# A first load of b as two loads of one slice each, and a first cast shared by two engines, in a matmul-GELU-matmul kernel on Trainium2

## The chip, the cores and the metric

The kernel runs on one core of one Trainium2 chip. That core has a matrix engine (PE, with its weight loads shown apart as PEld), a vector engine (DVE, VectorE), a scalar engine (ACT, ScalarE), GpSimd (POOL) and a sync engine (SP), each with an instruction queue of its own, and DMA engines that move data between the chip's memory (HBM) and the core's memory. Instructions of different queues are ordered by semaphores only. The metric is the device time of one execution in microseconds (us). The kernel before the change takes 117.73 us, the median of three runs that lie between 117.45 and 117.9 us.

## What is computed

```python
def reference(a, b, c):                     # a 1024x1024, b 1024x2048, c 2048x1024, float32
    h = np.matmul(a, b)
    h = 0.5 * h * (1 + np.tanh(np.sqrt(2 / np.pi) * (h + 0.044715 * h ** 3)))
    return np.matmul(h, c).astype(np.float32)
```

## The kernel before

The kernel keeps h transposed, as two halves `hT[0]` and `hT[1]` of 512 rows of a each. For that it needs a transposed (`aT`, bf16, by half h and by contraction slice k of 128; there are eight slices) and b in bf16 (`b1` for its first 1024 columns, `b2` for the rest). A matmul takes a slice of b, 128x128, as its weights and a slice of `aT`, 128x512, as the moving operand, and adds up the eight slices in one bank of PSUM.

The work has three parts. The first (lines 229 to 287) makes the first four column tiles of h for both halves with plain matmuls. The other columns of h and the whole second product go through `seven`, a Strassen-like scheme with seven block products in place of eight, whose sums VectorE and ScalarE work out. The last part writes the output, in tiles of 128 rows by 512 columns, through `store` (line 428).

The change touches the start. There, five loads are issued on SP's queue (lines 75 to 79), in this order: a's first quarter of columns for half 0 (`sta[:, 0, 0]`, 512 KB), b's contraction slices 0 and 1 (`stb[:, 0:2]`, 512 KB in one load), a's first quarter for half 1 (`sta[:, 1, 0]`, 512 KB), a's second quarter for half 0 (`sta[:, 0, 1]`, 512 KB), and b's slice 2 (`stb[:, 2]`, 256 KB). They arrive as float32. All further loads go through GpSimd's queue (lines 85 to 104), which casts to bf16 on the way; GpSimd issues none of them before it has copied one element of the first load of a (`gate`, line 81). While nothing has arrived, the matrix engine multiplies zeros (`stir`, line 122).

The order on each engine is the order of the program, written out by hand. Around the change it is this:

- `cast_a(0, 0, nc.vector)` (line 230) casts a's first load into a bf16 tile `ab`, in one VectorE instruction for all 256 columns (line 110).
- `turn(0, 0, 4, ab)` (lines 138 to 147) makes two steps, one for each contraction slice n: four 128x128 transposes on the matrix engine (line 145), then one VectorE copy of the result into `aT` (line 146). The generator is advanced with `next(tn)`, so that other work can be put between its steps.
- `cast_b(0, nc.vector, nc.vector, nc.scalar)` (line 233) casts b's slice 0 in three pieces of columns, of 128, 128 and 256; `cast_b(1, nc.scalar)` (line 236) casts slice 1 in one ScalarE instruction (line 108).
- `cast_a(1, 0, nc.vector, nc.scalar)` (line 237) casts a's load for half 1 in two pieces of 128 columns, VectorE's for the first slice and ScalarE's for the second.
- `block(0, range(4), (0,))` and `block(0, range(2), (1,))` (lines 238 and 239) are six matmuls (line 114). Then come the eight transposes for half 1 (line 240), and so on slice by slice, alternating with loads that GpSimd has brought.

The change also touches the end of the program text: `done2` (line 431) stores an output tile in one transfer of 256 KB or in two of 128 KB. Before, the tiles j = 1 and j = 2 of the first group, (i, l) = (0, 0), go in two. With five loads and 19 stores, SP issues 24 transfers. Tiles named `ot` that wait to be stored share four buffers (line 302).

Of the kernel before, what the change touches and what calls it, by code (L numbers as in the profile page):

```python
# [19 lines left out]
def kernel(ctx, tc, a, b, c, out):  # L20
    nc = tc.nc
# [3 lines left out]
    H = 512  # L25
# [4 lines left out]
    bv = b.rearrange("(kt p) n -> p kt n", p=128)  # L30
# [9 lines left out]
    def slot(tag, shape, dt, name):  # L40
        return big.tile(shape, dt, name=name, tag=tag)

    def bank(i, shape=(128, H), dt=F32, name="ps"):
        return pp.tile(list(shape), dt, name=name, tag=f"bank{i}", padded_shape=None)

    def pieces(tag, bufs, shape, dt, name):
        return small.tile(shape, dt, name=name, tag=tag, bufs=bufs)
# [17 lines left out]
    stb = slot("x0", [128, KT, H], F32, "stb")  # L65
# [3 lines left out]
    def a_part(h, q):  # L69
        return av[:, 4 * h:4 * h + 4, ds(q * 256, 256)]  # L70

    def b_part(q):
        return bv[:, 2 * q:2 * q + 2, 0:H]

    nc.sync.dma_start(out=sta[:, 0, 0], in_=a_part(0, 0))  # L75
    nc.sync.dma_start(out=stb[:, 0:2], in_=b_part(0))  # L76
    nc.sync.dma_start(out=sta[:, 1, 0], in_=a_part(1, 0))
    nc.sync.dma_start(out=sta[:, 0, 1], in_=a_part(0, 1))
    nc.sync.dma_start(out=stb[:, 2], in_=bv[:, 2, 0:H])
# [19 lines left out]
    for n in range(2):  # L99
        for k in range(0, KT, 4):  # L100
            nc.gpsimd.dma_start(out=b2[:, k:k + 4, ts(n, H)],
                                in_=bv[:, k:k + 4, ds(1024 + n * H, H)])
# [3 lines left out]
    def copy(eng, dst, src):  # L106
        if eng is nc.scalar:
            nc.scalar.activation(dst, src, AF.Copy)
        else:
            nc.vector.tensor_copy(dst, src)  # L110
# [11 lines left out]
    def stir(*widths):  # L122

        for w in widths:
            nc.tensor.matmul(ps[0, 3][:, 0:w], warm[:, 0:128], warm[:, 0:w],
                             start=True, stop=True, skip_group_check=True)

    def cast_a(h, q, *engs):

        ab = pieces("ab", 2, [128, 4, 256], BF16, "ab")  # L130
        for i, eng in enumerate(engs):
            w = 256 // len(engs)
            for j, e in enumerate(eng if isinstance(eng, tuple) else (eng,)):
                m = slice(2 * j, 2 * j + 2) if isinstance(eng, tuple) else slice(0, 4)
                copy(e, ab[:, m, ts(i, w)], sta[:, h, q][:, m, ts(i, w)])
        return ab

    def turn(h, q, i, ab):

        banks = i if isinstance(i, tuple) else (i,)  # L140
        pts = [bank(x, (128, 2, H), BF16, "pt") for x in banks]
        for n in range(2):
            pt = pts[n % len(pts)]
            for m in range(4):
                nc.tensor.transpose(pt[:, n, ts(m, 128)], ab[:, m, ts(n, 128)], ident)  # L145
            nc.vector.tensor_copy(aT[:, h, 2 * q + n], pt[:, n])  # L146
            yield
# [79 lines left out]
    one = Seven(4, quarters(b2, 0, H), BB, [None] * 4, zero.t)  # L227

    stir(256, 256, 256, 256, 256)
    tn = turn(0, 0, 4, cast_a(0, 0, nc.vector))  # L230
    next(tn)
    stir(128)
    cast_b(0, nc.vector, nc.vector, nc.scalar)
# [15 lines left out]
    tn = turn(0, 1, 7, ab)  # L249
# [4 lines left out]
    for q in range(1, 3):  # L254
        k = 2 * q
        block(0, range(4), (k,))
        tn = turn(1, q, 7, abq[:, q, 1])
# [5 lines left out]
        tn = turn(0, q + 1, 7, abq[:, q + 1, 0])  # L263
# [10 lines left out]
    tn = turn(1, 3, 0, abq[:, 3, 1])  # L274
# [153 lines left out]
    def store(mt, q0, w, ot, eng=None):  # L428
        (eng or nc.sync).dma_start(out=out[ts(mt, 128), ds(q0, w)], in_=ot)

    def done2(i, l, j, p):
        if (i, l) == (1, 0):
            ot = pieces("o", 4, [128, H], F32, "ot")
            nc.vector.tensor_copy(ot, p)
            p = ot
        n = 2 if (i, l) == (0, 0) and j else 1
        for q in range(n):
            r = ds(q * (H // n), H // n)
            store(4 * i + j, l * H + q * (H // n), H // n, p[:, r])

    def between2(n):
# [12 lines left out]
        elif n == "P73":  # L454
            two.t4(two.t[1], 4)

    seven(two, done2, between2)


# [28 lines left out]
```

## Time and profile before

| what | value |
|---|---|
| time, median of three runs (lowest, highest) | 117.73 us (117.45, 117.9) |
| span of the profiled execution, first to last instruction | 115.7 us |
| median time less that span | 2.0 us |
| matrix engine busy | 111.1 us, 96% of the span |
| VectorE, ScalarE, GpSimd busy | 90.0, 51.4, 17.2 us |
| granted clock of the matrix engine | 1.000 |
| first instruction that uses a's first load | 4.40 us |
| first product matmul | 6.83 us |

The profile is of one execution. Its page gives the span of that execution, 115.7 us, but no time of its own for what lies around the span; the table therefore sets the span beside the median of the runs. Times inside a profile count from the start of the span. A line of the timeline gives start, duration, engine, source line, operation, the tile written and the tile read, and in brackets how long the engine had been idle and what ended that. The chain of waits follows the work that ended last back to the start. Rows by window give, after the length, the busy time and the number of instructions of PE, PEld, DVE, ACT and POOL in that stretch, then the granted clock, the mean share of the DMA engines in use, and the GB/s moved.

### The profile page before, as it was taken

What the parts mean: (1) busy time and instruction counts of PE and PEld (TensorE: products, weight loads), DVE (VectorE), ACT (ScalarE), POOL (GpSimd) and SP (SyncE); (2) the same over time, 40 slices, a digit from 0 to 9 for tenths busy, and PEclk for the clock granted to TensorE, in tenths of its full rate; (3) what the DMA queues carried; (4) which work ended last, traced back from release to release, by engine and by line L of the source; (5) the groups of instructions that cost most, each with busy time, mean ns of one, the idle gap of its engine ahead of it and who ended that gap; (6) DMA issues with size and microseconds to landing.
All of it is one profiled execution on the core that took longest, in us unless ns stands there. A gap on an engine that the chain in (4) does not pass through costs nothing.

```text
span 115.7 us, 1461 instructions
## 1 busy us (share of the span) xinstructions
PE 111.1 (96%) x542; PEld 77.1 (67%) x542; DVE 90.0 (78%) x107; ACT 51.4 (44%) x86; POOL 17.2 (15%) x29
## 2 busy tenths in 40 slices
PE   7989999999999999999999999999999999999980
PEld 6645555546776447888885444688888888888860
DVE  0347748789999998935699999999999986954770
ACT  5053000999259997166698429500124982000000
POOL 2497755223322000000000000000000000000000
PEclk9999999999999999999999999999999999999999
DMA  2999999999999999998000000060000002014993
GB/s 69 295 381 229 200 199 205 204 208 205 206 211 209 212 213 209 212 210 168 8 0 0 6 0 0 38 235 0 0 0 0 0 4 91 1 73 176 370 363 106
DMA packets 13414, 15.94 MB, mean 138 GB/s; under 512 B 736, under 2 KB 9312, under 8 KB 13408
## 3 DMA queue, kind: packets, MB, share of 16 engines
q0 software_dynamic: 8672, 9.31, 47.6%
q1 hardware_dynamic: 4736, 6.56, 15.8%
q8 instruction: 4, 0.07, 0.3%
q14 instruction: 2, 0.02, 0.0%
HBM read 20.97 MB, written 4.19 MB: 218 GB/s over the span
## 4 chain that ended last, share of the span: by engine, by line
PE 90%; DMA 5%; SPq 1%; DVE 1%; issue 0%
PE ps L212 76%; PE ps L114 11%; DMA sta<-in_a_dram 5%; PE pt L145 3%; SPq L76 0%; DVE ab L110 0%; SPq L75 0%; DVE ot L375 0%
## 5 line engine op out<-in xcount | busy, mean ns | idle before, releaser
L212 PE MATMUL ps<-x,s 128*128 128x512 f32 x128 | 29.6, 391 | 0.0
L212 PEld LDWEIGHTS ps<-x,s 128*128 128x128 f32 x128 | 24.0, 188 | 5.1
L212 PE MATMUL ps<-x,x 128*128 128x512 f32 x96 | 22.9, 394 | 0.0
L212 PEld LDWEIGHTS ps<-x,x 128*128 128x128 f32 x96 | 18.0, 188 | 3.9
L114 PE MATMUL ps<-aT,b 128*128 128x512 bf16 x64 | 16.1, 379 | 0.2 <-DVE b L110 0.2
L298 ACT ACTIVATE v<-ps 128x512 f32<-128x512 f32 x10 | 6.0, 599 | 19.1 <-PE ps L212 19.1
L212 PE MATMUL ps<-c_sb,hT 128*128 128x512 bf16 (+1 forms) x72 | 14.2, 356 | 0.0
L212 PE MATMUL ps<-x 128*128 128x512 f32 x56 | 13.2, 392 | 0.0
L212 PEld LDWEIGHTS ps<-x 128*128 128x128 f32 x56 | 10.2, 188 | 2.6 <-ACT u L298 0.4
L118 ACT ACTIVATE hT<-ps 128x512 bf16<-128x512 f32 x14 | 7.3, 595 | 9.7 <-PE ps L114 9.7
L212 PEld LDWEIGHTS <-hT 128*128 128x128 bf16 x72 | 6.9, 98 | 7.0 <-issue 0.5
L118 ACT ACTIVATE hT<-ot 128x512 bf16<-128x512 f32 x18 | 10.4, 624 | 2.0 <-DVE ot L303 2.0
L212 PE MATMUL ps<-aT,b 128*128 128x512 bf16 x48 | 10.7, 379 | 0.0
L146 DVE COPY aT<-pt 128x512 bf16<-128x512 bf16 x16 | 6.7, 423 | 5.1 <-PE pt L145 5.1
L303 DVE TENSOR_TENSOR ot<-ps,u 128x512 f32<-128x512 f32 x10 | 6.7, 690 | 5.1 <-ACT u L298 5.1
L303 DVE TENSOR_TENSOR ot<-ps,v 128x512 f32<-128x512 f32 x10 | 6.7, 688 | 4.8 <-DMA out_dram<-ot 3.8
L170 DVE TENSOR_TENSOR x<-c_sb 128x1024 fp32r<-128x1024 bf16 x8 | 9.3, 1226 | 0.0
L114 PEld LDWEIGHTS <-b 128*128 128x128 bf16 x64 | 5.7, 98 | 4.5 <-DVE b L110 0.3
L212 PEld LDWEIGHTS <-b 128*128 128x128 bf16 x48 | 4.6, 98 | 5.7 <-issue 0.3
L104 POOL DMA_DIRECT2D c_sb<-in_c_dram x8 | 5.6, 702 | 13.1 <-DMA b<-in_b_dram 12.4
L170 DVE TENSOR_TENSOR x<-b 128x1024 fp32r<-128x1024 bf16 (+1 forms) x4 | 7.0, 1752 | 0.6 <-issue 0.6
L298 ACT ACTIVATE u<-ps 128x512 f32<-128x512 f32 x10 | 5.9, 598 | 3.4 <-PE ps L212 3.2
(44 smaller groups left out, 111.3 us busy)
## 6 DMA issues: line engine op xcount, KB each, us to landing
c_sb<-in_c_dram POOLq DMA_DIRECT2D x8, 512.0 KB, 20.0
out_dram<-ot SPq DMA_DIRECT2D x13, 256.0 KB, 2.1
b<-in_b_dram POOLq DMA_DIRECT2D x6, 512.0 KB, 15.3
sta<-in_a_dram SPq DMA_DIRECT2D x3, 512.0 KB, 6.1
abq<-in_a_dram POOLq DMA_DIRECT2D x5, 256.0 KB, 7.9
out_dram<-ot SPq DMA_DIRECT2D x6, 128.0 KB, 2.0
stb<-in_b_dram SPq DMA_DIRECT2D x1, 512.0 KB, 5.3
b<-in_b_dram POOLq DMA_DIRECT2D x2, 256.0 KB, 8.2
```

The lines of the kernel that those rows point to most:

```text
L104: nc.gpsimd.dma_start(out=c_sb[:, t:t + 2], in_=cv[:, t:t + 2])
L114: nc.tensor.matmul(p, b1[:, k, ts(t, 128)], aT[:, h, k], start=(k == 0), stop=(k == KT - 1))
L118: nc.scalar.activation(hT[h][:, t], p, AF.Gelu_apprx_tanh)
L145: nc.tensor.transpose(pt[:, n, ts(m, 128)], ab[:, m, ts(n, 128)], ident)
L146: nc.vector.tensor_copy(aT[:, h, 2 * q + n], pt[:, n])
L170: nc.vector.tensor_tensor(out=dst[:, r], in0=x[:, r], in1=y[:, r], op=op)
L212: nc.tensor.matmul(p[:, ds(c0, w)], l[:, k, ts(j, 128)], r[:, k, ds(c0, w)], start=(start and k == 0), stop=(k == self.kt - 1), skip_group ...
L298: nc.scalar.activation(st, p, AF.Copy)
L303: nc.vector.tensor_tensor(out=ot, in0=p, in1=st, op=ADD)
```

## The change

```diff
     nc.sync.dma_start(out=sta[:, 0, 0], in_=a_part(0, 0))
-    nc.sync.dma_start(out=stb[:, 0:2], in_=b_part(0))
+    for k in range(2):
+        nc.sync.dma_start(out=stb[:, k], in_=bv[:, k, 0:H])
     nc.sync.dma_start(out=sta[:, 1, 0], in_=a_part(1, 0))
...
-    tn = turn(0, 0, 4, cast_a(0, 0, nc.vector))
+    tn = turn(0, 0, 4, cast_a(0, 0, nc.vector, nc.scalar))
...
-        n = 2 if (i, l) == (0, 0) and j else 1
+        n = 2 if (i, l, j) == (0, 0, 1) else 1
```

b's slices 0 and 1 come in two loads of 256 KB, one behind the other, in the place of the one of 512 KB; each has its own semaphore, so that slice 0 can be used before slice 1 is there. a's first load is cast in two pieces of 128 columns, the first by VectorE and the second by ScalarE, where it was one VectorE instruction of 256 columns. The output tile j = 2 of the first group is stored in one transfer in the place of two, so SP still issues 24 transfers: six loads and 18 stores.

## The prediction

> **What bounds the kernel now.** I read the chain of waits first, because the change sits in the first 8 us of a span of 115.7 us, and only a chain tells whether those count. Its pieces in order of time:
>
> ```profile
> 1.24 0.50 SPq L76
> 1.73 0.05 issue
> 1.78 6.10 DMA sta<-in_a_dram
> 7.88 0.02 issue
> 7.90 0.44 DVE ab L110
> 8.34 0.05 issue
> 8.38 0.62 PE pt L145 x8
> ...
> 24.46 87.96 PE ps L212 x400
> ```
>
> From 8.38 us on there is nothing but the matrix engine up to 112.42. So a change at the start moves the time only by moving 8.38. What ends last before it is not b's load, which the change splits, but a's load for half 1 (line 77): in use at 7.90, cast in 0.44, transposed at 8.38.
>
> The timeline from 4 to 8.5 us says the same from the side of the matmuls:
>
> ```profile
> 4.40 0.69 DVE L110 CAST ab<-sta 128x1024 bf16<-128x1024 f32 x1 [4.40 <-DMA sta<-in_a_dram]
> ...
> 6.54 0.36 DVE L110 CAST b<-stb 128x128 bf16<-128x128 f32 x2 [0.53 <-DMA stb<-in_b_dram]
> 6.83 1.47 PE L114 MATMUL ps<-aT,b 128*128 128x512 bf16 x6 [0.15 <-DVE b L110]
> 7.90 0.43 DVE L110 CAST ab<-sta 128x512 bf16<-128x512 f32 x1 [0.67 <-DMA sta<-in_a_dram]
> ...
> 8.38 0.62 PE L145 MATMUL pt<-ident,ab 128*128 128x128 bf16 x8
> ```
>
> The six matmuls that wait for b end at 6.83 + 1.47 = 8.30, and the transposes behind them on the same queue start at 8.38. They just fit in.
>
> Next question: what sets the arrival at 7.90? Rows by window, the last two numbers the DMA engines' share and the GB/s:
>
> ```profile
> 3.25:3.75 0.50, 0.50 (x3) 0.41 (x2) 0.00 (x0) 0.00 (x0) 0.00 (x0) 1.00 1.12 377
> 3.75:4.25 0.50, 0.50 (x2) 0.40 (x2) 0.00 (x0) 0.00 (x0) 0.00 (x0) 1.00 0.73 236
> 4.25:5.75 1.50, 1.43 (x9) 0.84 (x8) 0.86 (x2) 0.00 (x0) 1.32 (x2) 1.00 0.97 272
> 5.75:7.25 1.50, 1.11 (x9) 0.76 (x8) 0.95 (x4) 0.71 (x2) 1.50 (x4) 1.00 1.06 368
> 7.25:8.75 1.50, 1.41 (x12) 0.66 (x11) 0.43 (x1) 0.85 (x2) 1.50 (x3) 1.00 1.11 396
> ```
>
> The DMA engines are full from 4.25 on. SP issues the five loads within 0.74 to 3.38 us; they are in use at 4.40, 6.54, 7.90, 9.42 and 9.98, about 1.4 us per 512 KB later on. The loads stand in line; it is bytes that a's second load waits for, not its issue. One thing stands out: b's own stretch, 3.75 to 5.75, runs at some 263 GB/s, where the stretches behind it run at 368 and 396.
>
> GpSimd's loads come behind these: in the DMA view from 5.2 to 9 us all packets are on the sync queue, though GpSimd issued its first load at 5.08. And the matrix engine has little to spare there. Its own timeline, and below it that of its weight loads:
>
> ```profile
> 15.07 1.03 PE L114 MATMUL ps<-aT,b 128*128 128x512 bf16 x4
> 15.93 0.39 PE L145 MATMUL pt<-ident,abq 128*128 128x128 bf16 x4
> ```
>
> ```profile
> 15.88 0.26 PEld L145 LDWEIGHTS <-abq 128*128 128x128 bf16 x4 [0.28 <-DMA abq<-in_a_dram]
> ```
>
> The weight load of those transposes waits 0.28 us for a GpSimd load and starts at 15.88; the matrix engine is free at 15.93. So only 0.05 us could be gained at 8.38 without the whole line of loads moving too.
>
> **The change, part by part.**
>
> *Cast of a's first load in two pieces.* Out goes one VectorE cast of 0.69 us; in come a VectorE cast of 128x512 (the row at 7.90: 0.43) and a ScalarE cast of the same size (0.63 in the row of that engine at 7.90), side by side. They end at 4.83 and 5.03 instead of 5.09. The stirs hold the matrix engine to 0.78 + 4.30 = 5.08 (first group of the timeline), so the first transposes move from 5.15 to about 5.10. ScalarE is idle then (4.30 us before 6.54), so its piece costs nothing. GpSimd's one-element copy lasted 0.70 us, from 4.43 to 5.13, as long as the VectorE cast beside it; if it follows the shorter cast, GpSimd issues 0.26 us earlier, into the same line behind the sync queue: 0.
>
> *Slice 0 of b on its own.* b's bytes move from about 3.75 to 5.75 and are in use 0.79 us after that. Half the bytes are there at 4.75, so slice 0 is in use near 5.55. VectorE is then copying the first transposes (5.5 to 5.95, 0.42 each), and casts slice 0's two pieces in 0.36 behind it. The first matmul starts near 6.15, 0.7 us earlier than 6.83. Slice 1 is in use at 6.54 as before, ScalarE's cast of it takes 0.61, and the two matmuls on it follow near 7.2 and are done at about 7.8 (0.59 for two, as in the row at 8.84 of the matrix engine). Then the matrix engine waits for a's second load until 8.38. The wait of 0.08 us (8.30 to 8.38) becomes one of some 0.6, and the time gained for b is given back there: 0. VectorE's queue holds the copy of the second transposes behind the casts, done near 6.75, well ahead of 7.90. The cover that hides it all is a's second load; were that load 0.6 us earlier, the gain would be real.
>
> *One more issue on SP.* The new issue costs what line 79's load of one slice does, 0.55 us, plus 0.05 between issues: 0.60 for the three loads behind it. a's second load is issued at 2.38 instead of 1.78. The first load was issued at 0.74 and bytes flowed at 1.75 to 2.00 (41 GB/s), about 1.1 us later. So a's second load is ready near 3.5, and its turn in line comes at 5.75: margin 2.2 us, cost 0. The ends: 0, and 0.60 were it the issue that counts.
>
> *The line itself.* The trace holds no two loads of b one behind the other there. Lower end: a load of a single slice does run at full rate (line 79's lies in the stretch of 396 GB/s). Were b's slow stretch due to its two-slice form, 0.524 MB would take 1.42 us at 368 GB/s instead of 1.99 at 263, and everything behind would come 0.57 earlier. Upper end: one more turn from load to load. The turn from a's first load to b's cost (377 - 236)/377 x 0.5 us = 0.19; the turns later on show no dip. I take 0: the nearest row in place and data is b's own stretch, and GpSimd's two-slice loads of b show no sign that two slices are slow. The range keeps -0.57 and +0.19.
>
> *The store.* One issue of 256 KB replaces two of 128 KB near 76 us. The `ot` buffer it frees is not written again before 93.83, and landing takes 2.1 us for the one size and 2.0 for the other: 0. The last stores and the count of 24 are unchanged.
>
> The sum against the profiled execution: 115.7 + 0 - 0 = 115.7 us of span, with 2.0 us around it (117.73 - 115.7; the profile gives no time of its own for that execution): 117.7.
>
> *Rules of the Trainium skill.* The trace shows loads that overlap: line 79's 256 KB land 7.1 us after their issue but are in use only 0.56 us after the load ahead of them (9.98 against 9.42). The page "DMA: Bandwidth & Descriptors", section "Anatomy of one DMA — SWDGE (gpsimd) path", puts a fixed cost of about 2.0 us on each DMA, and its section on measured bandwidth says to batch to at least 1 MiB; paid in line, that rule would make this change 2.0 us slower, 119.7. The measured 0.56 decides against it. The same page, section "Queues, rings and completion order", says that a DMA engine takes turns between queues packet by packet; the view from 5.2 to 9 us shows packets of the sync queue alone. By that rule an earlier GpSimd issue would cost the sync loads bandwidth.
>
> **The rivals.**
>
> 1. *b's load gets faster in two pieces* (117.16). For it: the slow 263 GB/s, and one-slice loads that do not show it. Against it: the stretch may be slow because of when it runs. If it holds, a's second load is in use at 7.33 and the transposes start at 7.81, just behind the matmuls (7.8, less what slice 1 gains too); GpSimd's loads follow, as they stand behind the sync queue. 117.73 - 0.57 = 117.16, 0.48% faster; if GpSimd's loads do not follow, 0.05 is left.
> 2. *The issue counts* (118.33, slower). The chain, read literally, goes from issue to issue on SP and then 6.10 us of load. If landing went by issue, the place is line 77 behind one more issue, the price 0.60: 117.73 + 0.60. It decides once a's second load is ready later than b's last byte, that is, if readiness slips by over 2.2 us from what I have, or b's bytes end before 3.5. Against it: full DMA engines.
> 3. *The change doesn't do what it says*: slice 0 is not in use before slice 1, because the two run mixed, or matmuls do not start before 6.83. The time would be 117.7 all the same.
>
> **How the numbers follow.** No change (with rival 3 in it, and with one more turn, 117.9): 0.57. Rival 1: 0.30. Rival 2 and its kind: 0.13. Within 0.5% is about what a measurement of this kernel can tell from no change: 117.14 to 118.32. Rival 1 centres on that edge, so half of its 0.30 lies beyond it: faster 0.15, within 0.57 + 0.15 = 0.72, slower 0.13. The range goes from rival 1, 117.1, to the turn's 117.9 plus the spread of the runs (117.9 - 117.45 = 0.45, of which I take 0.3): 118.2.
>
> **What would show it.** Slice 0's casts near 5.6 to 6.3 and the first product matmul near 6.15; the second matmuls' end near 7.8; a wait of the matrix engine for the cast of a's second load, which is still in use near 7.90; transposes at 8.38; an unbroken matrix engine from there. Rival 1 shows as b's stretch above 350 GB/s and that cast near 7.3; rival 2 as the cast near 8.5 and a DMA share that drops before it. The prediction is wrong if the line of loads moves in either direction, since nothing else here reaches 8.38.

## The result, and the profile after

The change made the kernel slower. Before: 117.58 us, median of 12 runs (117.45 to 118.04). After: 119.19 us, median of 12 runs (118.05 to 120.18). The ratio is 1.0093, 95% interval 1.007 to 1.0115, so about 117.58 x 1.0093 = 118.7 us; it leaves out the three longest runs of after (119.8 and above), whose granted clock is no lower than that of the others, and by the medians of all runs the ratio is 1.014. Forecast were 117.7 and a range that ended at 118.2.

After's runs do not lie around one value: their spans are 116.3 to 116.4, 116.7, 117.4 to 117.5 and 118.0 to 118.4 us. The profile is of one of the shortest executions (span 116.3, time 118.08), so it shows the smallest loss; run e4 below has the profile of a longer one.

The chain of waits of after, in order of time. The columns are start, length and what it was:

```profile
1.22 0.50 SPq L77
1.72 0.05 issue
1.77 0.42 SPq L77
2.19 0.04 issue
2.23 6.28 DMA sta<-in_a_dram
8.52 0.02 issue
8.54 0.44 DVE ab L111
8.98 0.05 issue
9.02 0.62 PE pt L146 x8
...
74.01 39.09 PE ps L213 x180
```

It is the chain of before with one more issue in it, and it ends on the same work: a's load for half 1, its cast, the transposes, and then the matrix engine to the end (113.10). From the transposes to that end it is 113.10 - 9.02 = 104.08 us; before it was 112.42 - 8.38 = 104.04. The whole difference of the two profiles, 116.3 - 115.7 = 0.6 us, is therefore the 0.64 by which the transposes start later.

The timeline of after, casts and matmuls from 4 to 9.6 us (start, length, engine, line, operation, in brackets how long the engine was idle and what ended that):

```profile
4.60 0.43 DVE L111 CAST ab<-sta 128x512 bf16<-128x512 f32 x1 [4.60 <-DMA sta<-in_a_dram]
4.60 0.63 ACT L109 ACTIVATE ab<-sta 128x512 bf16<-128x512 f32 x1 [2.35 <-DMA sta<-in_a_dram]
5.08 0.40 PE L146 MATMUL pt<-ident,ab 128*128 128x128 bf16 x4
6.35 0.36 DVE L111 CAST b<-stb 128x128 bf16<-128x128 f32 x2 [0.41 <-DMA stb<-in_b_dram]
6.64 1.04 PE L115 MATMUL ps<-aT,b 128*128 128x512 bf16 x4
7.18 0.63 ACT L109 ACTIVATE b<-stb 128x512 bf16<-128x512 f32 x1 [0.41 <-DMA stb<-in_b_dram]
7.86 0.60 PE L115 MATMUL ps<-aT,b 128*128 128x512 bf16 x2 [0.19 <-ACT b L109]
8.54 0.43 DVE L111 CAST ab<-sta 128x512 bf16<-128x512 f32 x1 [1.49 <-DMA sta<-in_a_dram]
9.02 0.62 PE L146 MATMUL pt<-ident,ab 128*128 128x128 bf16 x8 [0.56 <-DVE ab L111]
```

Slice 0 is in use at 6.35, only 0.19 ahead of where both slices were in use before (6.54). Slice 1 follows at 7.18, 0.64 later than before, and a's load for half 1 at 8.54, also 0.64 later than its 7.90. The matrix engine waits 0.56 us for it. The rows by window (the last two numbers are the share of the DMA engines and the GB/s) say where the time was lost:

```profile
3.75:4.25 0.50, 0.50 (x2) 0.40 (x2) 0.00 (x0) 0.00 (x0) 0.00 (x0) 1.00 1.04 287
4.25:5.75 1.50, 1.50 (x9) 0.84 (x8) 0.66 (x2) 0.63 (x1) 1.12 (x2) 1.00 0.86 183
5.75:7.25 1.50, 1.23 (x10) 0.85 (x9) 0.88 (x4) 0.49 (x2) 1.50 (x4) 1.00 0.87 311
7.25:8.75 1.50, 1.03 (x4) 0.11 (x2) 0.21 (x1) 0.77 (x2) 1.50 (x3) 1.00 1.09 384
```

b's stretch from 4.25 to 5.75 moves 183 GB/s where the one load moved 272, and the next 311 for 368. Behind that the rate is as before (384 for 396). The share is 0.86 for 0.97, so more time passes without packets, and single packets are slower: the longest that starts in this stretch takes 1.11 us, where before it was 0.32.

### The profile page after: what moved, and what is told of

Its sections match the earlier page's. It is cut to its first block, busy times and chain, and to the rows that moved or that the text cites. A ratio compares the mean times of both kernels' runs of the same rounds, so it can differ in the third digit from the quotient of the medians.

```text
span 116.3 us, 1458 instructions
## 1 busy us (share of the span) xinstructions
PE 111.0 (95%) x536; PEld 77.1 (66%) x542; DVE 89.7 (77%) x107; ACT 52.1 (45%) x87; POOL 17.0 (15%) x29
## 4 chain that ended last, share of the span: by engine, by line
PE 89%; DMA 5%; SPq 1%; DVE 1%; issue 1%
PE ps L213 75%; PE ps L115 11%; DMA sta<-in_a_dram 5%; PE pt L146 3%; SPq L77 1%; DVE ab L111 0%; DVE ot L376 0%; SPq L75 0%
```

## The experiments

**Which half of the change costs the time?**

e1 is after with the whole cast of a's first load kept on VectorE:

```diff
-    nc.sync.dma_start(out=stb[:, 0:2], in_=b_part(0))
+    for k in range(2):
+        nc.sync.dma_start(out=stb[:, k], in_=bv[:, k, 0:H])
...
-        n = 2 if (i, l) == (0, 0) and j else 1
+        n = 2 if (i, l, j) == (0, 0, 1) else 1
```

> The changed kernel with a's first load cast by VectorE alone again, so b's two loads and the single store of tile j = 2 are left. Theory A (the two loads of b move more slowly than the one did, and everything behind them in the line comes later): the whole loss is here, ratio to before 1.006 to 1.015, b's stretch from 4.25 to 5.75 us below 240 GB/s and a's second load in use near 8.5 us. Theory B (the cast in two pieces does it, because GpSimd's copy ends earlier and its loads come into the line sooner): ratio 1.00, a's second load in use near 7.9.

119.46 us, ratio 1.0119, interval 1.0082 to 1.0156. Without the cast in two pieces the loss is all there. This run still has the single store of tile j = 2, but after's whole difference lies ahead of 9.02 us, long before that store.

e2 is the cast alone:

```diff
-    tn = turn(0, 0, 4, cast_a(0, 0, nc.vector))
+    tn = turn(0, 0, 4, cast_a(0, 0, nc.vector, nc.scalar))
```

> The kernel before with a's first load cast by VectorE and ScalarE, and nothing else. Theory A: ratio 1.000 within 0.2%, transposes of half 1 near 8.38 us as before. Theory B: the whole loss, ratio 1.006 to 1.015.

117.74 us, ratio 1.0024, interval 1.0003 to 1.0046: small, but not nothing. Its timeline has the reason, a clash of two instructions:

```profile
4.73 0.88 POOL L86 DMA_DIRECT2D abq<-in_a_dram  x1
...
7.56 1.55 POOL L86 DMA_DIRECT2D abq<-in_a_dram  x2
7.84 0.78 DVE L110 CAST ab<-sta 128x512 bf16<-128x512 f32 x1 [0.50 <-DMA sta<-in_a_dram]
...
8.67 0.62 PE L145 MATMUL pt<-ident,ab 128*128 128x128 bf16 x8 [0.20 <-DVE ab L110]
```

GpSimd's first issue starts at 4.73 (5.08 before), so a later one, begun at 7.56, is 0.28 us under way when VectorE's cast on the chain begins at 7.84. That cast takes 0.78 us instead of 0.43, and the transposes start at 8.67 instead of 8.38.

e15 keeps the cast in two pieces, but lets GpSimd's one-element copy read the end of ScalarE's piece, so that GpSimd starts as late as before:

```diff
-    nc.gpsimd.tensor_copy(gate, sta[:, 0, 0, 3, 0:1])
...
+    ab0 = pieces("ab", 2, [128, 4, 256], BF16, "ab")
+    nc.vector.tensor_copy(ab0[:, :, 0:128], sta[:, 0, 0][:, :, 0:128])
+    nc.scalar.activation(ab0[:, :, 128:256], sta[:, 0, 0][:, :, 128:256], AF.Copy)
+    nc.gpsimd.tensor_copy(gate, ab0[:, 3, 255:256])
...
-    tn = turn(0, 0, 4, cast_a(0, 0, nc.vector))
+    tn = turn(0, 0, 4, ab0)
```

> The kernel before with a's first load cast by VectorE and ScalarE, as in the kernel that had only that; but GpSimd's one-element copy, which lets its loads begin, reads the end of ScalarE's piece instead of a's load, so that GpSimd begins at about 5.0 to 5.1 us as before. If the 0.24% came from GpSimd beginning earlier and blocking VectorE's cast of a's second load, that cast takes 0.43 us again and the ratio is 0.999 to 1.001. If it came from something else, 1.002 to 1.003 again.

117.54 us, ratio 0.9999, interval 0.9989 to 1.001. In its timeline the cast is short again:

```profile
5.06 0.87 POOL L89 DMA_DIRECT2D abq<-in_a_dram  x1
...
7.90 1.53 POOL L89 DMA_DIRECT2D abq<-in_a_dram  x2
7.92 0.43 DVE L113 CAST ab<-sta 128x512 bf16<-128x512 f32 x1 [0.66 <-DMA sta<-in_a_dram]
```

The two instructions still overlap (7.90 and 7.92), but here they begin together. So the cast in pieces costs nothing, and e2's loss goes with GpSimd's earlier start. The other profiles of this case show the same: this cast took 0.43 us where it began within the first 0.15 us of a GpSimd issue (before, e9, e10), and 0.51 to 0.78 where it began 0.26 to 0.55 us into one (e2, e4, e5, e8, e12). In after it began 0.71 us into one and took 0.43, so this is no part of the loss in after's profile. The page "SBUF — State Buffer" of the Trainium skill, section "Who interferes with whom", describes a pair of memory ports that VectorE and GpSimd share as an exclusive lock, won by whoever issues first, with copies and casts among the VectorE operations that can need it. These times would agree with it if an issue held the lock only in its middle, which no run here shows.

**Is the loss the same each time?** e4 is after unchanged, for a second profile. Its edit is that of e1 and that of e2 together.

> The changed kernel once more, as it is, since its runs spread from 118.05 to 120.18 us where those of before spread from 117.45 to 118.04, and the one profile is of a run near the lower end (span 116.3). Theory A expects a profile of a longer run to show still slower loads of b, with a's second load in use 1 us or more after 8.5 and an unbroken matrix engine from there; the rival expects the same start and the loss later, between 9 us and the end.

119.52 us (118.58 to 121.26), ratio 1.0152, interval 1.0111 to 1.0193. The profile (span 118.1) shows the same fault, larger. Its timeline:

```profile
8.69 0.63 ACT L109 ACTIVATE b<-stb 128x512 bf16<-128x512 f32 x1 [1.88 <-DMA stb<-in_b_dram]
10.04 0.53 DVE L111 CAST ab<-sta 128x512 bf16<-128x512 f32 x1 [2.96 <-DMA sta<-in_a_dram]
...
11.94 0.42 ACT L109 ACTIVATE ab<-sta 128x256 bf16<-128x256 f32 x1 [1.28 <-DMA sta<-in_a_dram]
...
12.41 0.40 PE L146 MATMUL pt<-ident,ab 128*128 128x128 bf16 x4
```

and two of its rows by window:

```profile
3.75:4.25 0.50, 0.50 (x2) 0.39 (x2) 0.19 (x1) 0.19 (x1) 0.16 (x1) 1.00 0.92 164
4.25:5.75 1.50, 1.50 (x9) 0.97 (x8) 0.42 (x2) 0.44 (x1) 1.50 (x3) 1.00 0.85 130
```

130 GB/s in b's stretch; slice 1 in use at 8.69 (7.18 in the other profile), a's load for half 1 at 10.04 (7.90 before), a's next at 11.94 (9.42 before). The transposes for that one start at 12.41, where before it was 9.94: 2.47 later, and the span is 118.1 - 115.7 = 2.4 longer. So in the two profiles that there are, the loss of after sits in one place and varies in size.

The trace also has the moment at which each of the 16 DMA engines finished its part of a load. b's one load before: first engine 5.95, last 6.52. b's second load in after's profile: 5.42 and 7.15. In e4: 5.50 and 8.66. The first engine is done no later, but a load can be used only when its last engine is. And the load behind it comes late by just as much: its last engine finishes a's load for half 1 at 7.88, 8.52 and 10.01, each time 1.35 to 1.37 us after the last one of b. b's last engine is 0.64 us late in after and 2.15 in e4, and a's load for half 1 is 0.64 and 2.14 late. That is the whole loss of the line, with nothing left for the later issue of a's load.

**Is it the place in SP's line (rival 2), or two loads as such?** e17 and e18 take the load of slices 0 and 1 off SP's queue and issue it from ScalarE's at the start, as one load and as two (e18 with the other parts of after):

```diff
-    nc.sync.dma_start(out=stb[:, 0:2], in_=b_part(0))
+    nc.scalar.dma_start(out=stb[:, 0:2], in_=b_part(0))
```

```diff
-    nc.sync.dma_start(out=stb[:, 0:2], in_=b_part(0))
+    for k in range(2):
+        nc.scalar.dma_start(out=stb[:, k], in_=bv[:, k, 0:H])
...
-    tn = turn(0, 0, 4, cast_a(0, 0, nc.vector))
+    tn = turn(0, 0, 4, cast_a(0, 0, nc.vector, nc.scalar))
...
-        n = 2 if (i, l) == (0, 0) and j else 1
+        n = 2 if (i, l, j) == (0, 0, 1) else 1
```

> The kernel before, whose first load of b is issued on ScalarE's queue at the start in the place of SP's, so that it runs beside a's first load and not behind it. If the slowness of b's first read is waiting, which other packets can fill, both loads are in use by 5.9 us, a's second load near 7.4, and the ratio is 0.995 to 1.000. If it is lost time of the DMA engines wherever it stands, a's first load is in use near 6, a's second load near 7.9 or later, ratio 1.000 to 1.006.

> The changed kernel with b's two loads issued on ScalarE's queue in the place of SP's. If two loads of b cost only in the line behind a's first load, this one is like the last one, within 0.3%. If two loads cost wherever they stand, it is slower than the last one by 0.5% or more.

The times, 121.07 us (1.029, 1.0264 to 1.0315) and 120.59 us (1.0229, 1.0205 to 1.0252), say little about the loads, since in both the first product waits long enough that the matrix engine's clock falls (below). The arrivals do. SP issues a's load for half 1 at 1.22 in e17 and at 1.23 in e18. Timeline of e17, then of e18:

```profile
6.09 0.93 ACT L108 ACTIVATE b<-stb 128x256 bf16<-128x256 f32 x2 [3.33 <-DMA stb<-in_b_dram]
6.40 0.69 DVE L110 CAST ab<-sta 128x1024 bf16<-128x1024 f32 x1 [6.40 <-DMA sta<-in_a_dram]
...
7.71 0.63 ACT L108 ACTIVATE ab<-sta 128x512 bf16<-128x512 f32 x1 [0.68 <-DMA sta<-in_a_dram]
```

```profile
7.43 0.43 DVE L111 CAST ab<-sta 128x512 bf16<-128x512 f32 x1 [7.43 <-DMA sta<-in_a_dram]
...
8.93 0.63 ACT L109 ACTIVATE b<-stb 128x512 bf16<-128x512 f32 x1 [0.56 <-DMA stb<-in_b_dram]
...
9.49 0.63 ACT L109 ACTIVATE ab<-sta 128x512 bf16<-128x512 f32 x1
```

Against what was expected, e18 is the faster of the two. With the same issue on SP, though, a's first load comes 1.03 later, b's second slice 2.84 later and a's load for half 1 up to 1.78 later; from 2 to 4 us the engines move 151 GB/s for 247. So rival 2, though its sign was there (a cast at 8.54, a DMA share of 0.86), is not the cause: here nothing on SP was issued later, in e4 the cost, 2.14, is over three times the 0.60 of an issue, and a's load for half 1 followed b's last engine at the same distance as before.

**Is it b's load alone that suffers from a split?** e8 splits it the other way, into column halves that hold both slices; e12 leaves b whole and splits a's load for half 1. Both make up for it at the stores as after does.

```diff
-    nc.sync.dma_start(out=stb[:, 0:2], in_=b_part(0))
+    for q in range(2):
+        nc.sync.dma_start(out=stb[:, 0:2, ts(q, 256)], in_=bv[:, 0:2, ts(q, 256)])
```

```diff
-    nc.sync.dma_start(out=sta[:, 1, 0], in_=a_part(1, 0))
+    for m in range(0, 4, 2):
+        nc.sync.dma_start(out=sta[:, 1, 0, m:m + 2], in_=a_part(1, 0)[:, m:m + 2])
```

> The kernel before, with b's first load split by columns instead of slices: two loads, each of both slices and 256 columns, so every row piece is 1 KB as in a's loads, where it was 2 KB; tile j = 2 is stored in one transfer. If two loads in the place of one are what costs, ratio 1.006 to 1.015 as for the changed kernel. If the size of a row piece or the rows that the 16 DMA engines read at one time matter, the rate of the stretch differs from both kernels: 350 GB/s or more and a ratio of 0.995 to 1.000 if 1 KB pieces are read as smoothly as a's.

> The kernel before with a's load for half 1 in two loads of 256 KB (two of its four row blocks each) and b's load whole; tile j = 2 is stored in one transfer. If a further load in the line costs in itself, ratio 1.006 or more; if only the splitting of b's load does, ratio 0.999 to 1.002, a's second load in use near 7.9 us.

e8: 119.39 us, 1.0116 (1.0068 to 1.0165), a's load for half 1 in use at 9.54; of the second half of b, 14 engines were done by 6.48, the last two at 7.56 and 8.09. e12: 118.04 us, 1.0039 (1.0024 to 1.0054); in its profile, of its longest run, a's load for half 1 is in use at 8.62, 0.72 late, and its VectorE cast takes 0.77, as in e2. So it is neither the split by slices nor b alone: an extra load came with a later arrival in each of the three ways in which it was tried. How e12's 0.39% divides between the arrival and the cast in its other runs is not shown.

**Why was b's stretch slow already with one load?** If that were understood, the cost of two might follow. e3 moves b's load behind a's for half 1:

```diff
-    nc.sync.dma_start(out=stb[:, 0:2], in_=b_part(0))
     nc.sync.dma_start(out=sta[:, 1, 0], in_=a_part(1, 0))
+    nc.sync.dma_start(out=stb[:, 0:2], in_=b_part(0))
```

> The kernel before with the second and the third load on SP's queue exchanged: a's load for half 1 goes ahead of b's first load, which stays one load. Two readings of the slow stretch from 3.75 to 5.75 us. If it belongs to b's first load, a's second load runs at 350 GB/s or more and is in use near 6.0 us, and b's load runs at some 265 GB/s behind it and is in use near 8.0. If it belongs to the second place in the line, whatever stands there, a's second load is in use near 6.5 and b's near 7.9, at 350 GB/s or more. Time by either: the six matmuls now come last and are not hidden, start near 8.3, ratio 1.005 to 1.012.

121.46 us, 1.0287 (1.0239 to 1.0335). Its rows by window; the last three numbers are the granted clock, the share of the DMA engines and the GB/s:

```profile
3.75:5.00 1.25, 1.25 (x4) 0.76 (x4) 0.69 (x1) 0.00 (x0) 0.75 (x2) 1.00 1.06 368
5.00:7.00 2.00, 1.54 (x13) 1.11 (x12) 0.42 (x1) 0.00 (x0) 2.00 (x3) 1.00 0.85 221
...
8.50:9.00 0.50, 0.00 (x0) 0.00 (x0) 0.20 (x2) 0.20 (x1) 0.50 (x2) 0.76 0.89 320
9.00:12.00 3.00, 2.62 (x7) 1.02 (x8) 1.22 (x4) 2.39 (x6) 1.73 (x3) 0.50 1.31 245
12.00:12.50 0.50, 0.50 (x10) 0.50 (x9) 0.03 (x1) 0.00 (x0) 0.00 (x0) 0.82 1.41 199
```

a's load now runs at 368 GB/s in the place where b's was slow, and b's is slow (221) where a's was fast. So, in this one profile, it is b and not the place. (The time is lost elsewhere: b is in use at 8.80 only, the matrix engine idles 2.60 us and then works at half clock.)

Is it the first read of b, its rows, or their distance of 8 KB? e7 fetches slices 6 and 7 in place of 0 and 1; e9 fetches from c, whose rows are 4 KB long; e10 fetches from c so that the 2 KB pieces of a slice lie side by side; e6 loads slice 2 ahead of slices 0 and 1; e5 first reads 64 bytes of each of the 256 rows on ScalarE's queue. e7, e9, e10 and later e11 leave b's slices 0 and 1 out of the product for the first 512 columns.

e7:

```diff
-    nc.sync.dma_start(out=stb[:, 0:2], in_=b_part(0))
+    nc.sync.dma_start(out=stb[:, 0:2], in_=b_part(3))
```

> The kernel before, whose first load of b fetches slices 6 and 7 in the place of 0 and 1, in the same form and place; so slices 0 and 1 are left out of the product for the first 512 columns of b, and the others count as before. Theory F, and any theory of the form of the load: the stretch stays below 280 GB/s, ratio 1.00. A theory of the rows themselves (slices 0 and 1 lie badly): 350 GB/s or more, a's second load in use near 7.4, ratio 0.995.

e9:

```diff
-    nc.sync.dma_start(out=stb[:, 0:2], in_=b_part(0))
+    nc.sync.dma_start(out=stb[:, 0:2], in_=cv[:, 0:2, 0:H])
```

> The kernel before, whose first load of b fetches the same number of pieces of 2 KB from c instead, whose rows lie 4 KB apart as a's do, where b's lie 8 KB apart; so slices 0 and 1 of b are left out for the first 512 columns and other numbers stand in for them. If the distance of the rows in HBM makes the stretch slow, it runs at 330 GB/s or more, a's second load is in use near 7.4 us, ratio about 0.995. If it does not matter, the stretch stays at 230 to 270 GB/s, ratio 1.00.

e10:

```diff
-    nc.sync.dma_start(out=stb[:, 0:2], in_=b_part(0))
+    near = c.rearrange("(kt p2) (x q) -> (p2 x) kt q", p2=64, x=2)
+    nc.sync.dma_start(out=stb[:, 0:2], in_=near[:, 0:2])
```

> As the last one, with the pieces of 2 KB of a slice side by side in c, so that a slice is 256 KB without gaps; the same part of the product is left out. If the distance of the rows matters: 350 GB/s or more, as good as the last one or better, ratio about 0.995. If not: 230 to 270 GB/s, ratio 1.00.

e6:

```diff
     nc.sync.dma_start(out=sta[:, 0, 0], in_=a_part(0, 0))
+    nc.sync.dma_start(out=stb[:, 2], in_=bv[:, 2, 0:H])
...
-    nc.sync.dma_start(out=stb[:, 2], in_=bv[:, 2, 0:H])
```

> The kernel before with the load of b's slice 2 (256 KB) moved ahead of the load of slices 0 and 1. Theory F: slice 2, which ran at full rate in the fifth place, is now slow (under 280 GB/s), and the load of slices 0 and 1 behind it is at 350 or more. Theory S: slice 2 keeps its rate and slices 0 and 1 stay at some 265 GB/s. By either, a's second load is in use 0.7 us later or more, ratio 1.005 to 1.015.

e5, which stores one tile in one transfer to keep 24:

```diff
+    touch = consts.tile([128, 2, 16], F32, name="touch")
+    nc.scalar.dma_start(out=touch, in_=bv[:, 0:2, 0:16])
```

> The kernel before, with one small load on ScalarE's queue ahead of everything: the first 16 numbers (64 bytes) of each of the 256 rows that b's first load will read; nothing uses them. The store of tile j = 2 goes in one transfer, which keeps 24. Theory F (whatever is read from b first is slow, because it is the first read): b's load runs at 350 GB/s or more, a's second load is in use near 7.4 us, ratio 0.995 or a little above for the time the small load itself takes. Theory S (it is something in these rows of b, in how they lie, or in the form of the load): b's stretch stays below 280 GB/s and the ratio is 1.000 to 1.005.

| run | time, us | ratio (95% interval) | GB/s, 4.25 to 5.75 | a's load for half 1 in use |
|---|---|---|---|---|
| before | 117.58 | 1 | 272 | 7.90 |
| e7, other slices of b | 117.62 | 0.9996 (0.9981, 1.0011) | 233 | 7.83 |
| e9, c, rows 4 KB apart | 117.69 | 1.0021 (1.0005, 1.0037) | 210 | 7.95 |
| e10, c, side by side | 117.95 | 1.0028 (1.0006, 1.0051) | 367 | 7.28 |
| e5, rows touched first | 117.76 | 1.0024 (1.0007, 1.0041) | 262 | 8.63 |
| e6, slice 2 first | 120.74 | 1.0255 (1.022, 1.0291) | 133 (3.75 to 5.75) | 9.92 |

In e6 slice 2, fast in before, is slow where it comes first, though there two loads of b also follow one another. Only e10 is fast, and there b's slice 2, now the first read of b, ran at 253 GB/s (7.75 to 9.00) and was in use at 9.92. So the slow thing is a first read of b or c whose 2 KB pieces lie apart, whichever rows they are; touching the rows does not cure it (e5's row is from the profile of a run of 118.28, above its median). Lying apart is not enough by itself: a's loads, in pieces of 1 KB that lie 4 KB apart, ran at 368 to 377. Why, these runs don't tell.

e10 answers another question besides: a's load for half 1 was there 0.62 earlier, yet the span is 115.8. Its chain of waits:

```profile
4.39 0.65 POOL gate L82
5.04 6.28 DMA abq<-in_a_dram
11.32 0.29 issue
11.61 0.73 POOL b L99
12.35 12.96 DMA b<-in_b_dram
25.30 0.84 issue
26.15 1.24 DVE x L171
```

Now GpSimd's loads end last. A faster load on SP is worth nothing here unless they move too.

**Does the second load cost as much where there is no slow first read?** e11 is e10 in two loads; e16 and e13 put a load of b's slices 6 and 7 ahead of all others and then load slices 0 and 1 in one and in two; e14 is e13 with that load from c.

Stores are merged so that 24 transfers remain. e11:

```diff
-    nc.sync.dma_start(out=stb[:, 0:2], in_=b_part(0))
+    near = c.rearrange("(kt p2) (x q) -> (p2 x) kt q", p2=64, x=2)
+    for k in range(2):
+        nc.sync.dma_start(out=stb[:, k], in_=near[:, k])
```

> As the last one, in two loads of one slice each as in the changed kernel, with the one store of tile j = 2; the same part of the product is left out. If it is the distance of b's rows that makes the two loads slow, this one is no slower than before: ratio 0.995 to 1.001. If two small loads in this place are slow in themselves, whatever they read, ratio 1.006 to 1.015, with single engines that lag by 1 us as in the changed kernel.

e16, and e13 with the two loads of e1 as well:

```diff
+    nc.sync.dma_start(out=stb[:, 6:8], in_=b_part(3))
     nc.sync.dma_start(out=sta[:, 0, 0], in_=a_part(0, 0))
```

> As the first of these, with slices 6 and 7 of b read ahead, but b's slices 0 and 1 in one load as before. If two loads cost only because b is read for the first time, this one and the kernel with two loads differ by less than 0.2%, and both stretches run at 350 GB/s or more. If two loads cost in themselves, this one is faster by 0.5% or more.

> The kernel before with b's first load in two as in the changed kernel, and a further load of 512 KB (slices 6 and 7 of b, which nothing uses) on SP's queue ahead of all others, so that b has been read once when the two loads come; all tiles of the first group are stored in one transfer, which keeps 24. Everything starts some 2 us later, ratio 1.015 to 1.03. If the first read of b is what is slow, the two loads now run at 350 GB/s or more, with few long packets, and land within 0.8 us of each other's first engine; if two loads are slow in themselves, their stretch stays under 250 GB/s.

e14, also with the two loads of e1:

```diff
+    nc.sync.dma_start(out=stb[:, 6:8], in_=cv[:, 6:8, 0:H])
     nc.sync.dma_start(out=sta[:, 0, 0], in_=a_part(0, 0))
```

> As the last one, but the further load reads 512 KB of c in the same form, so b is still unread when its two loads come. If the first read of b is what is slow, the two loads stay under 250 GB/s and the kernel is slower than the last one by 0.5 us or more; if a load ahead is enough (a warm queue, whatever it read), the two kernels are the same.

The rows of e10 and then of e11 for the stretch in which b's place is loaded show that the second load slows even pieces that lie side by side, 259 GB/s for 367:

```profile
4.25:5.75 1.50, 1.50 (x9) 0.98 (x8) 0.74 (x2) 0.06 (x1) 1.36 (x2) 1.00 1.01 367
4.25:5.75 1.50, 1.27 (x9) 0.70 (x8) 0.88 (x2) 0.42 (x1) 1.34 (x2) 1.00 0.87 259
```

Times: e11 117.81 us, 1.0028 (1.0004 to 1.0052); e16 120.92, 1.0301 (1.0264 to 1.0339); e13 120.87, 1.0287 (1.0249 to 1.0324); e14 120.59, 1.0233 (1.0214 to 1.0252). The last three carry a load more ahead of everything, so they are read by arrivals. From the first use of a's first load to that of a's load for half 1, 1 MB passes in every kernel:

| what is loaded between | one load | one load more | difference, us |
|---|---|---|---|
| b, first read | 3.50 (before; e7 3.53; e9, from c, 3.65) | 3.94 (after), 5.98 (e4) | +0.44, +2.48 |
| the same, by columns | 3.50 (before) | 5.33 (e8) | +1.83 |
| the same, a's load split instead | 3.50 (before) | 4.51 (e12) | +1.01 |
| c, side by side | 2.92 (e10) | 3.49 (e11) | +0.57 |
| b, read before | 2.68 (e16) | 3.20 (e13) | +0.52 |

Every pair has the sign. Counted from the start of the span, a's load for half 1 is later by 0.64, 2.14, 1.64, 0.72, 0.59 and 0.35 us. But each entry is one profile: the five kernels with one load of pieces that lie apart and nothing ahead of it (before, e2, e7, e9, e15) spread by 0.17, and e5, with one load of b and its small load ahead, has 4.04.

The times do not repeat the sign in the last two rows. e11 has the same ratio as e10, and e13 is no slower than e16, where 0.5% was expected if two loads cost in themselves. So a cost in time is shown for the slow first read, where it is large and uneven; without it, a delay of the arrival by 0.35 to 0.59 us shows in one pair of profiles each, and no cost in time. In e10 GpSimd's loads end last and would hide such a delay; in e16 and e13 the clock falls, and what hides it is not shown.

e14 has 3.00 with b unread, less than after's 3.94, so the load that runs ahead matters too, even if it isn't of b. How much of it is the first read and how much the early phase remains open, and so does what holds back the last DMA engine.

No version beat both kernels.

## Why the prediction was wrong, by its own steps

- **What bounds the kernel: right.** 8.38 moved to 9.02 and the end moved with it, over a matrix engine that pauses for 0.05 us at most. The wait of some 0.6 us ahead of the transposes came out as well (0.56), but by luck, since both its ends moved: the second matmuls ended at 8.46 and not 7.8. That nearly nothing could be gained at 8.38 alone was right too (e10).
- **The line itself: this is the step that failed.** "Upper end: one more turn from load to load" was put at 0.19 us, and "I take 0". The term measures +0.64 in the profiled execution of after and +2.14 in e4. The price came from the turn from a's first load to b's, read as a dip of the rate. What a second load costs does not show there: it is the time until the slowest DMA engine has finished, and in the slow read that engine finished 1.73 to 3.16 us after the first (0.57 before), with the load on the chain right behind it. What holds that engine back stays open.
- **The estimate from the slow stretch leaned the wrong way.** The lower end, -0.57, assumed that two slices in one load were the slow form. b's stretch was slow in every form tried with pieces that lie apart, and slower in two loads.
- **Slice 0 on its own: late.** Half the bytes at 4.75 and use near 5.55 took for granted that 263 GB/s stays. Use was at 6.35 and the first product matmul at 6.64, not 6.15.
- **The cast in two pieces: right in itself (e15), but "GpSimd issues 0.26 us earlier ...: 0" was wrong.** Alone it cost 0.24% (e2), through VectorE's cast on the chain and not through the DMA line that the step looked at.
- **Issue, margin 2.2 us, cost 0: holds as far as shown.** The issue itself cost 0.45 us (2.23 for 1.78), not 0.60, and with unchanged issues on SP the delay appears all the same (e18).
- **The rivals.** Rival 1 didn't occur. Rival 2 had the right sign, its cast "near 8.5" came at 8.54, and its 118.33 lies among after's runs; that is chance, since the mechanism is another. Rival 3 did not hold: slice 0 was used ahead of slice 1.
- **The range** ended at 118.2, below rival 2's own 118.33, since the bound of the unknown cost was taken from a row that shows only the middle of a load and not its last engine. Two loads one behind the other were not in the trace, so the rows could not exclude one of the size of 0.6.

## What to carry to other kernels

A load is there when its slowest DMA engine is done, and the rate in the middle of one load does not tell when two in its place would be: here the split cost 0.6 to 2.1 us, in the first read of a tensor whose pieces lie apart. Before splitting a load to start sooner, look at what the chain waits for behind it: there the later arrival was paid in full, while the early start was worth nothing. And when an instruction off the chain moves earlier, ask which later instruction of its engine now overlaps one on the chain.

## What the runs showed of the hardware that was not expected

- Reading b for the first time, its stretch runs at 130 to 272 GB/s in nearly every place and with whichever rows (303 in e14, behind a load of c), and, from 5.50 to 7.50, at 387 in one load (e16) and 346 in two (e13) when other rows of b were read just before; 2 KB pieces that lie side by side run at 367 to 391 at once in one load (e10), but at 259 from 4.25 to 5.75 in two (e11).
- The clock of the matrix engine fell after short idling. In e3 the engine had nothing to do from 6.78 on (9.38 - 2.60); the row from 8.50 to 9.00 has a mean of 0.76 between rows of 1.00 and 0.50, so the clock halved near 8.76, after some 2.0 us, and the row from 12.00 to 12.50, at 0.82, puts its return near 12.18. Six matmuls then took 2.74 us instead of 1.47. In e1's profile it halved near 10.74 (0.74 in the row from 10.50 to 11.00), though the longest idle stretch just before was 1.24 us and matmuls ran from 9.19 to 9.79. The page "TensorE: Matmul & The Clock Gate" of the Trainium skill, section "Part 1: The HAM clock gate", gives free-running windows of 3413 ns, and half clock after at least one idle window of about 3.4 us. The 3.42 us at half clock in e3 (8.76 to 12.18) agree with the window; the idling before the fall was shorter here.
- The same program, after, gave spans of 116.3 to 119.5 us in 18 runs (e4's included; the longest at a granted clock of 0.986), where before gave 115.5 to 116.4 in the 96 runs beside the experiments. In the two profiles of after it is how late the last DMA engine is that differs.
